# A decoder block on one core: choice weights' exponentials held together on ScalarE, their sums behind the first block's choice, and expert rows shared out anew between the stages

## The chip, the cores and the metric

The kernel runs on one core of one Trainium2 chip, in one launch. The metric is the device time of an execution in microseconds (us). A core has a TensorE (PE) for matrix products, a VectorE (DVE), a ScalarE (ACT), a GpSimd (POOL) and a SyncE (SP) that only issues transfers; each of them works through its own instructions in order and waits for the others by semaphores.

## What is computed

The block takes 512 tokens of 1024 channels. Its first half is three token mixers side by side (forgetting attention, sliding-window attention, attention to 256 memory rows), gated and merged. Its second half, where the change lies, is a retrieval of single-neuron experts:

```python
def peer_ffn(h, w_q, keys1, keys2, u, v):
    q = (h @ w_q).astype(jnp.float32).reshape(B, S, PEER_HEADS, 2, half)
    s1 = jnp.einsum('bshd,hkd->bshk', q[..., 0, :], keys1)
    s2 = jnp.einsum('bshd,hkd->bshk', q[..., 1, :], keys2)
    v1, i1 = lax.top_k(s1, PEER_TOPK)
    v2, i2 = lax.top_k(s2, PEER_TOPK)
    cand = (v1[..., :, None] + v2[..., None, :]).reshape(...)
    sv, si = lax.top_k(cand, PEER_TOPK)
    experts = e1 * N_KEYS + e2          # e1, e2: the keys behind the 16 best sums
    gates = jax.nn.softmax(sv, axis=-1)
    a = jnp.einsum('cd,ced->ce', h_c, u[e_c])
    act = jax.nn.gelu(a) * g_c
    out = jnp.einsum('ce,ced->cd', act, v[e_c])
```

Each token thus has 8 heads x 16 = 128 of 16384 experts, each with a row of u and a row of v (1024 floats).

## The kernel before

The tokens are four blocks of 128. Blocks 0 and 1 fetch their experts' rows by indirect DMA: a "row" is one expert slot for all 128 tokens of a block, a gather of 512 KB issued by POOL (L868). There are 512 of them in a fixed order: 128 u rows and 128 v rows of block 0, then the same of block 1. The function `step` handles one row and issues gathers for a few rows ahead. A u row is a product with the token and a sum on DVE (L883); a v row is scaled and added to an accumulator on DVE, which lies in SBUF (`mg`, L890) for rows beside the mixers and in PSUM (`two`, L893 and L896) for all later ones. Some rows are handled "apart": a v row is scaled on ACT (L886) and added on POOL (L887).

Blocks 2 and 3 are "dense": all 128 tiles of u and of v go through PE, and the gates are spread out to all 16384 experts. The stages follow each other like this:

1. Block 0's mixers and search; then the mixers of blocks 1 to 3, with block 0's rows beside them until `EARLY_ROWS` are done. These rows have a low priority.
2. The search of blocks 1 to 3 (`search`, L711 to L757). PE forms queries and scores of 8 heads in two halves each, 16 halves in all (scores: L754, copied to SBUF by ACT at L757); the splits `wlo` of the query weights are made by POOL (L129); POOL adds up candidates (L722); DVE finds the best 16 of three blocks for each half and then of the candidates. One row is handled each time the costs that `search` yields have added up to `PER_ROW`; every `APART`-th of them goes apart while less than `NO_APART` is spent.
3. The choice. PE runs the u tiles k=4 to 31 of the dense blocks (`dense_u`, L1029, with ACT's Gelu at L1031), with two PSUM banks. `weigh` makes the gates of blocks 1 to 3: DVE subtracts the best score (L781), ACT takes three exponentials (L784), DVE sums, inverts and multiplies (L788 to L791). `choose` finds the expert numbers of block 2, then 3, then 1, on DVE, with a row for each unit of cost (`AMONG`).
4. The spread (L1089 to L1107): 64 turns, with 60 rows among them, and u tiles. It begins with the turn of block 2's numbers and gates on PE (L1076).
5. The dense loop: 128 turns of a v tile (12 products of 512 columns), u tiles 57 to 127, and all rows that are left, shared out evenly over the first 124 turns.

Up to the end of the search a scheduler orders the instructions of all engines by its own estimate of their times. From there on POOL, DVE and PE keep the order of the code, and ACT is still ordered by the scheduler, except where `keep_in_program_order` holds an instruction.

The credit that `PER_ROW` is compared with is the same variable that `pump` sets to zero when no side work is left (L87 to L93), and each of the search's 16 weight loads calls `pump`:

```python
                cost = next(side[0], None)
...
            if cost is None:
                credit[0] = 0.0
                break
```

Of the kernel before, what the change touches and what calls it, by code (L numbers as in the profile page):

```python
# [12 lines left out]
AF = mybir.ActivationFunctionType  # L13
# [11 lines left out]
GROUPS = ((0,), (1, 2, 3))  # L25
BIG = 3
DENSE = (2, 3)
# [23 lines left out]
UNREAD = 36  # L51
LATER = 400
PACE = {"search": 20.0, "choose": 8.0, "rows": 3.5}
EARLY_ROWS, PER_ROW, APART, NO_APART = 183, 4.2, 3, 94.0


@with_exitstack
def tile_block(ctx: ExitStack, tc: tile.TileContext, t: dict, out: bass.AP):
    nc = tc.nc
    V, A, PE, G = nc.vector, nc.scalar, nc.tensor, nc.gpsimd  # L60
# [622 lines left out]
    x1, gate, acts, eidx, chosen, h2n = {}, {}, {}, {}, {}, {}  # L683
    rstd = ep.tile([128, NB], F32, name="rstd")
# [92 lines left out]
    def weigh(pool, f, g):  # L777

        nb = len(GROUPS[g])
        ex = pool.tile([128, nb, PH, TOPK], F32, name="ex")  # L780
        V.tensor_sub(ex, f.best, f.best[:, :, :, 0:1].to_broadcast([128, nb, PH, TOPK]))  # L781
        for b in range(nb):
            bf = ex[:, b].rearrange("p h s -> p (h s)")
            A.activation(bf, bf, AF.Exp, scale=rstd[:, GROUPS[g][b]:GROUPS[g][b] + 1])  # L784
        yield 0.4
        den = small.tile([128, BIG * PH], F32, tag="gden", name="gden", bufs=1)[:, :nb * PH]
        dv = den.rearrange("p (b h) -> p b h", b=nb)
        V.reduce_sum(dv, ex, axis=AX.X)  # L788
        V.reciprocal(den, den)
        for b in range(nb):  # L790
            V.tensor_mul(gates_of[g][:, b].rearrange("p s h -> p h s"), ex[:, b],  # L791
                         dv[:, b, :, None].to_broadcast([128, PH, TOPK]))
        yield 1.0

    def iota_of(pool):
        x = pool.tile([128, TOPK * NJ // 2], F32, name="iota_k")
        nc.sync.dma_start(x, t["c_iota_k"])
        return x.bitcast(BF16).rearrange("p (k s) -> p k s", k=TOPK)

    def choose(bp, f, lb, iota_k, dst):  # L800

        def new(tag, dt=F32):
            return bp.tile([128, PH, TOPK], dt, tag=tag, name=tag)

        sh, p3, p2, ri, rj = new("sh", U32), new("p3"), new("p2"), new("ri"), new("rj")
        V.tensor_scalar(sh, f.pos[:, lb], 3, None, op0=OP.logical_shift_right)
        V.tensor_scalar(p3, sh, -1.0, 0.0, op0=OP.add, op1=OP.max)
        V.tensor_scalar(sh, f.pos[:, lb], 2, None, op0=OP.logical_shift_right)
        V.tensor_copy(p2, f.pos[:, lb])
        yield 0.6  # L810
        V.scalar_tensor_tensor(p3, sh, -6.0, p3, op0=OP.add, op1=OP.max)
        V.scalar_tensor_tensor(ri, p2, -48.0, p3, op0=OP.add, op1=OP.max)
        yield 0.4
        V.tensor_scalar(rj, ri, 4.0, 24.0, op0=OP.mult, op1=OP.add)
        V.tensor_scalar(p3, ri, 8.0, 8.0, op0=OP.mult, op1=OP.add)
        V.scalar_tensor_tensor(rj, ri, 16.0, rj, op0=OP.mult, op1=OP.min)
        yield 0.6
        V.scalar_tensor_tensor(rj, ri, 48.0, rj, op0=OP.add, op1=OP.min)
        V.tensor_tensor(rj, rj, p3, op=OP.min)
        V.tensor_sub(rj, p2, rj)  # L820
        for i, r in enumerate((ri, rj)):
            yield 0.6
            rb = bp.tile([128, TOPK, PH], BF16, tag="rb", name="rb")
            V.tensor_copy(rb, r.rearrange("p h s -> p s h"))
            idb = bp.tile([128, TOPK, PH], BF16, tag="idb", name="idb")
            V.tensor_copy(idb, f.ids[i][:, lb].rearrange("p h k -> p k h"))
            hot = bp.tile([128, TOPK, TOPK, PH], BF16, tag="hot", name="hot")
            hv = hot.rearrange("p k s h -> p k (s h)")
            V.tensor_tensor(hv, rb.rearrange("p s h -> p (s h)")[:, None, :].to_broadcast([128, TOPK, NJ]),
                            iota_k, op=OP.is_equal)  # L830
            yield 1.6
            V.tensor_tensor(hot, hot, idb[:, :, None, :].to_broadcast([128, TOPK, TOPK, PH]), op=OP.mult)
            yield 1.4
            for n in (8, 4, 2):
                V.tensor_add(hv[:, :n], hv[:, :n], hv[:, n:2 * n])
            V.tensor_add(dst[i], hv[:, 0], hv[:, 1])
            yield 1.4

    def numbers_of(pool, f, lb, b, iota_k):

        g2r = pool.tile([128, D], F32, name="g2r")
        row = t["g2_row"]
        nc.sync.dma_start(g2r, bass.AP(tensor=row.tensor, offset=row.offset, ap=[[0, 128], [1, D]]))
        e = [pool.tile([128, NJ], F32, tag=f"e{i}", name=f"e{i}") for i in range(2)]
        yield from choose(pool, f, lb, iota_k, e)
        V.scalar_tensor_tensor(e[0], e[0], float(NK), e[1], op0=OP.mult, op1=OP.add)
        V.tensor_copy(eidx[b], e[0])
        if b == 0:
            h2n[0] = h2n[1] = ep.tile([128, D], F32, tag="own", name="own")
        V.scalar_tensor_tensor(h2n[b], x1[b], rstd[:, b:b + 1], g2r, op0=OP.mult, op1=OP.mult)  # L850
        yield 1.3
# [52 lines left out]
    def beside():  # L904
# [20 lines left out]
        with tc.tile_pool(name="ca", bufs=1, side="right") as pool:  # L925
            iota_k = iota_of(pool)
            yield from weigh(pool, f, 0)
            yield from numbers_of(pool, f, 0, 0, iota_k)
# [77 lines left out]
    def dense_u(k):  # L1006

        if k >= FIRST_U:
            fetch_u_to(min(max(k, PRE_U) + URING - 1, LAG) if k < LAG else k)
        w = u_raw.pop(k)  # L1010
        if split_u(k):
            if k % 2:
                hi, lo = (gp[0].tile([128, D], F32R, tag=tag, name=tag, bufs=1) for tag in ("uhi", "ulo"))
            else:
                hi, lo = halves_u[0][:, 0], halves_u[0][:, 1]
            A.copy(hi, w)
            yield
            V.tensor_sub(lo, w, hi.bitcast(F32))
            yield
            ps, hi, lo = bank("mm"), *(x.rearrange("p (n w) -> p n w", n=KC) for x in (hi, lo))  # L1020
            for dc in range(KC):
                mm3(ps[:, :TD], (hi[:, dc], lo[:, dc]), [x[dc] for x in h2s], dc == 0, dc == KC - 1)
            A.activation(ga(k), ps[:, :TD], AF.Gelu)
            return
        w = w.rearrange("p (n w) -> p n w", n=KC)
        yield
        ps = bank("mm")
        for dc in range(KC):
            PE.matmul(ps[:, :TD], w[:, dc], h2f[dc], start=dc == 0, stop=dc == KC - 1)  # L1029
            yield  # L1030
        A.activation(ga(k), ps[:, :TD], AF.Gelu)  # L1031

    f = Found(found, BIG)
# [26 lines left out]
    cp = build.enter_context(tc.tile_pool(name="cp", bufs=1))  # L1060
# [8 lines left out]
    iota_k = iota_of(cp)  # L1069

    def turn_block(i):

        ps = turned
        b = DENSE[i]
        for k, src in enumerate((*chosen[b], gate[b])):
            PE.transpose(ps[:, k * 128:(k + 1) * 128], src, ident)  # L1076
        eT = sp.tile([128, 3, 128], F32, tag="eT", name="eT", bufs=2)
        A.copy(eT.rearrange("p a b -> p (a b)"), ps[:, :384])
        slots[i] = eT
# [96 lines left out]

    NBAT = ND * 128 // GT
    PER = 128 // GT
    while k_u < FIRST_U + COVER:
        if k_u == FIRST_U + UNWEIGHED:  # L1180
            list(weigh(cp, f, 1))
        list(dense_u(k_u))
        k_u += 1
    ahead[0] = AHEAD + MORE
    credit[0] = 0.0
    for job in (*(choose(cp, f, lb, iota_k, chosen[DENSE[lb - 1]]) for lb in (1, 2)), numbers_of(cp, f, 0, 1, iota_k)):
        for cost in job:
            credit[0] += cost
            while credit[0] >= AMONG and done[0] < known[0]:
                credit[0] -= AMONG  # L1190
                step()
# [11 lines left out]
    for n in range(AHD, NBAT + AHD):  # L1203
# [8 lines left out]
        while credit[0] >= 1.0 and done[0] < known[0]:  # L1212
            credit[0] -= 1.0
            step(apart=done[0] % 4 == 0)
        if (n + 4) % PER == 0 and n + 4 < NBAT:
            turn_block((n + 4) // PER)
        spread(n - AHD)
# [139 lines left out]
```

## Time and profile before

| | us |
|---|---|
| median of 3 runs (lowest, highest) | 1583.12 (1581.81, 1583.77) |
| the profiled execution | 1584.12 |
| its span in the profile | 1582.3 |
| PE busy | 1512.7 (96%) |
| DVE busy | 1422.0 (90%) |
| ACT busy | 819.9 (52%) |
| POOL busy | 789.2 (50%) |
| transfers | 531.90 MB, mean 336 GB/s |

The profile is one execution recorded by the chip. Busy time is the union of an engine's instructions; a group names the line of the code, the engine, the tile written and the tiles read. In a timeline each row has its start and length, how many instructions it merges (x), and in brackets how long the engine was idle before and what released it. PE is near full in every stage, so single waits of a few us at the borders between stages are what such a profile is searched for.

### The profile page before, as it was taken

What the parts mean: (1) busy time and instruction counts of PE and PEld (TensorE: products, weight loads), DVE (VectorE), ACT (ScalarE), POOL (GpSimd) and SP (SyncE); (2) the same over time, 40 slices, a digit from 0 to 9 for tenths busy, and PEclk for the clock granted to TensorE, in tenths of its full rate; (3) what the DMA queues carried; (4) which work ended last, traced back from release to release, by engine and by line L of the source; (5) the groups of instructions that cost most, each with busy time, mean ns of one, the idle gap of its engine ahead of it and who ended that gap; (6) DMA issues with size and microseconds to landing.
All of it is one profiled execution on the core that took longest, in us unless ns stands there. A gap on an engine that the chain in (4) does not pass through costs nothing.

```text
span 1582.3 us, 27174 instructions
## 1 busy us (share of the span) xinstructions
PE 1512.7 (96%) x9458; PEld 1373.8 (87%) x9458; DVE 1422.0 (90%) x2661; ACT 819.9 (52%) x1831; POOL 789.2 (50%) x643
## 2 busy tenths in 40 slices
PE   8999899999999989999998999899999999999998
PEld 7989899998898989898787898688888888888887
DVE  6678487888999999999899999799999999999997
ACT  7778336646345533452215998554454454444442
POOL 1100015767576456977444665445555554555451
PEclk9999999999999999999999999999999999999999
DMA  8677657898998899987798999999999999999995
GB/s 319 212 252 251 236 197 251 307 368 310 326 348 309 280 342 337 321 307 250 240 401 303 375 396 386 347 399 390 408 409 409 410 410 407 408 406 404 408 409 193
DMA packets 178361, 531.90 MB, mean 336 GB/s; under 512 B 17456, under 2 KB 46384, under 8 KB 178224
## 3 DMA queue, kind: packets, MB, share of 16 engines
q0 software_dynamic: 73728, 268.47, 44.9%
q1 hardware_dynamic: 94416, 225.95, 39.3%
q10 hardware_dynamic: 10080, 35.75, 5.7%
q8 instruction: 74, 1.21, 0.3%
q14 instruction: 63, 0.52, 0.1%
HBM read 515.42 MB, written 14.68 MB: 335 GB/s over the span
## 4 chain that ended last, share of the span: by engine, by line
PE 58%; DVE 14%; issue 10%; DMA 10%; POOL 5%; ACT 2%; POOLq 0%; SPq 0%; DVEq 0%; ACTq 0%
PE mm L1029 9%; PE mm L146 9%; PE mm L145 9%; PE mm L147 9%; DMA row<-in_peer_v_dram,eidx 6%; POOL row L868 5%; PE sc L1104 3%; DVE two L896 2%; DVE wlo L131 2%; DMA row<-in_peer_u_dram,eidx 2%; PE sc L147 2%; PE sc L146 2%; PE tp L145 2%; PE tp L146 2%; PE sc L145 2%
## 5 line engine op out<-in xcount | busy, mean ns | idle before, releaser
L868 POOL DMA_INDIRECT row<-in_peer_v_dram,eidx x256 | 328.9, 1285 | 289.2 <-DVE two L896 164.1
L868 POOL DMA_INDIRECT row<-in_peer_u_dram,eidx x256 | 316.9, 1238 | 236.3 <-DVE scr L883 115.4
L131 DVE TENSOR_TENSOR wlo<-raw,whi 128x1024 fp32r<-128x1024 f32 (+1 forms) x228 | 278.1, 1221 | 34.2 <-ACT whi L119 30.0
L896 DVE SCALAR_TENSOR_TENSOR two<-row,acts,two 128x1024 f32<-128x1024 f32 x189 | 242.5, 1283 | 4.1 <-DMA row<-in_peer_v_dram,eidx 1.9
L119 ACT CAST whi<-raw 128x1024 fp32r<-128x1024 f32 x146 | 152.6, 1050 | 105.6 <-PE mm L146 59.7
L883 DVE SCALAR_TENSOR_TENSOR scr<-row,own 128x1024 bf16<-128x1024 f32 x128 | 156.2, 1220 | 19.0 <-DMA row<-in_peer_u_dram,eidx 17.9
L883 DVE SCALAR_TENSOR_TENSOR scr<-row,two 128x1024 bf16<-128x1024 f32 x116 | 140.9, 1215 | 5.1 <-DMA row<-in_peer_u_dram,eidx 4.3
L203 POOL TENSOR_TENSOR rsy<-rsv,mhalf 128x4 f32<-128x4 f32 (+5 forms) x25 | 38.6, 1546 | 185.6 <-DVE rsv L202 184.2
L1157 ACT CAST ah<-ga 128x256 fp32r<-128x256 f32 x116 | 47.0, 407 | 158.1 <-PE tp L146 123.8
L147 PE MATMUL mm<-hhi,wlo 128*128 128x384 f32 x320 | 110.6, 346 | 4.5 <-POOL wlo L129 4.5
L145 PE MATMUL mm<-hhi,whi 128*128 128x384 f32 x320 | 111.5, 348 | 1.6 <-ACT hhi L237 1.2
L146 PE MATMUL mm<-hlo,whi 128*128 128x384 f32 x320 | 111.9, 350 | 0.0
L1159 ACT CAST whi<-raw 128x1024 fp32r<-128x1024 f32 x96 | 100.3, 1047 | 16.1 <-DMA raw<-in_peer_v_dram 11.4
L146 PE MATMUL sc<-wlo,ah 128*128 128x512 f32 x256 | 101.2, 395 | 6.3 <-DVE wlo L131 6.3
L145 PE MATMUL mm<-whi,hhi 128*128 128x256 f32 (+1 forms) x360 | 103.7, 290 | 2.9 <-DVE g L604 1.9
L146 PE MATMUL mm<-wlo,hhi 128*128 128x256 f32 (+1 forms) x360 | 102.6, 286 | 1.5 <-DVE wlo L131 1.5
L147 PE MATMUL mm<-whi,hlo 128*128 128x256 f32 (+1 forms) x360 | 101.9, 285 | 0.8 <-DVE hlo L662 0.8
L147 PE MATMUL sc<-whi,al 128*128 128x512 f32 x256 | 101.6, 397 | 0.0
L145 PE MATMUL tp<-whi,ah 128*128 128x512 f32 x256 | 101.0, 395 | 0.0
L145 PE MATMUL sc<-whi,ah 128*128 128x512 f32 x256 | 101.0, 395 | 0.0
L146 PE MATMUL tp<-wlo,ah 128*128 128x512 f32 x256 | 100.9, 394 | 0.0
L147 PE MATMUL tp<-whi,al 128*128 128x512 f32 x256 | 100.6, 393 | 0.0
(323 smaller groups left out, 4527.8 us busy)
## 6 DMA issues: line engine op xcount, KB each, us to landing
raw<-in_peer_v_dram SPq DMA_DIRECT2D x96, 512.0 KB
hhi<-in_uT_dram ACTq DMA_DIRECT2D x68, 512.0 KB
raw<-in_w_tr_dram SPq DMA_DIRECT2D x48, 512.0 KB
raw<-in_w_nat_dram SPq DMA_DIRECT2D x40, 512.0 KB
last<-in_peer_v_dram SPq DMA_DIRECT2D x32, 512.0 KB
hhi<-in_uT_dram SPq DMA_DIRECT2D x26, 512.0 KB
raw<-in_w_o_dram SPq DMA_DIRECT2D x24, 512.0 KB
gd<-st SPq DMA_DIRECT2D x24, 512.0 KB
```

The lines of the kernel that those rows point to most:

```text
L119: (cast or A.copy)(hi[:, :n * w], raw[:, :n * w])
L131: V.tensor_sub(lo, raw, hi.bitcast(F32))
L145: PE.matmul(ps, lh, rh, start=first, stop=False)
L146: PE.matmul(ps, lh, rl, start=False, stop=False)
L147: PE.matmul(ps, ll, rh, start=False, stop=last)
L868: G.indirect_dma_start(out=r, out_offset=None, in_=t["peer_" + tab], in_offset=bass.IndirectOffsetOnAxis(ap=eidx[b][:, j:j + 1], axis=0))
L883: V.scalar_tensor_tensor(scr, r, 1.0, two[0] if b else h2n[b], op0=OP.mult, op1=OP.mult, accum_out=acts[b][:, c]))
L896: V.scalar_tensor_tensor(two[0], r, acts[b][:, c], two[0], op0=OP.mult, op1=OP.add))
L1029: PE.matmul(ps[:, :TD], w[:, dc], h2f[dc], start=dc == 0, stop=dc == KC - 1)
L1104: PE.matmul(ps[:, u], o[:, 1, u], o[:, 0, u], start=True, stop=True)
L1157: A.copy(ah, a)
L1159: A.copy(hi, raw)
```

## The change

Three edits:

- `EARLY_ROWS` goes from 183 to 176, `PER_ROW` from 4.2 to 3.4 and `APART` from 3 to 4.
- In `weigh`, the second and third exponential are held in program order on ACT, right behind the first.
- `weigh` is no longer run out at once. Its first part (the subtraction and the exponentials) stands where it stood, before u tile 18 in the code; its second part (sums, reciprocal, products) comes behind `choose` of block 2, and now counts as a cost for the rows.

```diff
-EARLY_ROWS, PER_ROW, APART, NO_APART = 183, 4.2, 3, 94.0
+EARLY_ROWS, PER_ROW, APART, NO_APART = 176, 3.4, 4, 94.0
...
-            A.activation(bf, bf, AF.Exp, scale=rstd[:, GROUPS[g][b]:GROUPS[g][b] + 1])
+            ins = A.activation(bf, bf, AF.Exp, scale=rstd[:, GROUPS[g][b]:GROUPS[g][b] + 1])
+            if b:
+                tc.keep_in_program_order(ins)
...
+    weighing = weigh(cp, f, 1)
     while k_u < FIRST_U + COVER:
         if k_u == FIRST_U + UNWEIGHED:
-            list(weigh(cp, f, 1))
+            next(weighing)
         list(dense_u(k_u))
         k_u += 1
...
-    for job in (*(choose(cp, f, lb, iota_k, chosen[DENSE[lb - 1]]) for lb in (1, 2)), numbers_of(cp, f, 0, 1, iota_k)):
+    for job in (choose(cp, f, 1, iota_k, chosen[DENSE[0]]), weighing, choose(cp, f, 2, iota_k, chosen[DENSE[1]]),
+                numbers_of(cp, f, 0, 1, iota_k)):
```

Because each weight load throws the credit away, the search does not get the 31 rows that 105.6 units of cost at 3.4 would give. Counted in the built programs, the rows are shared out so:

| rows | before | after |
|---|---|---|
| beside the mixers | 183 | 176 |
| in the search (DVE + apart) | 24 (17 + 7) | 26 (20 + 6) |
| in the choice, all on DVE | 36 | 37 |
| done when the spread begins | 243 | 239 |
| in the spread | 60 | 60 |
| left for the dense loop | 209 | 213 |

Line numbers of the changed kernel are higher by 2 behind L784 and by 4 behind L1188. All engines' orders are the same up to the start of the search. There, DVE before has seven of the rows beside the mixers (`mg<-row`) between the last work of the mixers and the first searches (MAX, MAX_INDEX and MATCH_REPLACE on the scores `s`); five of the seven are seen here:

```order
L1044 COPY rstd<-rsy 128x3
L890 SCALAR_TENSOR_TENSOR mg_2288<-row,acts_207,mg_2288 128x1024
L711 MAX v_7904<-s 128x8 x3
L712 MAX_INDEX ids_7609<-v_7904,s 128x8
L713 MATCH_REPLACE tmp<-v_7904,s 128x128
L890 SCALAR_TENSOR_TENSOR mg_2288<-row,acts_207,mg_2288 128x1024
L712 MAX_INDEX ids_7609<-v_7904,s 128x8 x2
L714 MAX v_7904<-tmp 128x8
L715 MAX_INDEX ids_7609<-v_7904,tmp 128x8
L890 SCALAR_TENSOR_TENSOR mg_2288<-row,acts_207,mg_2288 128x1024
L711 MAX v_7904<-s 128x8 x3
L890 SCALAR_TENSOR_TENSOR mg_2288<-row,acts_207,mg_2288 128x1024
```

On DVE at the same place in the changed kernel the first searches stand alone:

```order
L1046 COPY rstd<-rsy 128x3
L711 MAX v_7883<-s 128x8 x3
L712 MAX_INDEX ids_7588<-v_7883,s 128x8
L713 MATCH_REPLACE tmp<-v_7883,s 128x128
L712 MAX_INDEX ids_7588<-v_7883,s 128x8 x2
L714 MAX v_7883<-tmp 128x8
L715 MAX_INDEX ids_7588<-v_7883,tmp 128x8
L711 MAX v_7883<-s 128x8 x3
```

The seven rows are gone from there; the search has three more of the form `two<-row` on DVE, farther back, and one less apart.

On ACT, behind the search's last copy of scores, the exponentials (`ex<-ex`, each kind of function behind its ACT_TABLE_LOAD) stand among the Gelus of the u tiles (`ga<-mm`). Before:

```order
L757 COPY s<-sc 128x384
L886 ACTIVATE row<-row,acts_207 128x1024
L1031 ACTIVATE ga<-mm 128x256 x4
L784 ACT_TABLE_LOAD
L784 ACTIVATE ex<-ex,rstd 128x128
L1031 ACT_TABLE_LOAD
L1031 ACTIVATE ga<-mm 128x256
L784 ACT_TABLE_LOAD
L784 ACTIVATE ex<-ex,rstd 128x128 x2
L1031 ACT_TABLE_LOAD
L1031 ACTIVATE ga<-mm 128x256 x24
```

On ACT at the same place in the changed kernel:

```order
L757 COPY s<-sc 128x384
L888 ACTIVATE row<-row,acts_207 128x1024
L1033 ACTIVATE ga<-mm 128x256 x5
L784 ACT_TABLE_LOAD
L784 ACTIVATE ex<-ex,rstd 128x128 x3
L1033 ACT_TABLE_LOAD
L1033 ACTIVATE ga<-mm 128x256 x24
```

Two of the four table loads are gone, and one more Gelu, that of u tile 7, stands ahead of the exponentials.

On POOL in the second half of the search, the splits `wlo` of the query weights stand among gathers, candidates and rows apart (`mg<-mg,row`). Before:

```order
L129 TENSOR_TENSOR wlo<-raw,whi 128x1024
L868 DMA row<-in_peer_v_dram,eidx_206 128x1024 x3
L887 TENSOR_TENSOR mg_2288<-mg_2288,row 128x1024
L722 TENSOR_TENSOR cand<-v_8540 128x3x24
L722 TENSOR_TENSOR cand<-v_8540 128x3x16
L129 TENSOR_TENSOR wlo<-raw,whi 128x1024
```

On POOL at the same two splits in the changed kernel:

```order
L129 TENSOR_TENSOR wlo<-raw,whi 128x1024
L722 TENSOR_TENSOR cand<-v_8367 128x3x8
L889 TENSOR_TENSOR mg_2288<-mg_2288,row 128x1024
L870 DMA row<-in_peer_v_dram,eidx_206 128x1024
L722 TENSOR_TENSOR cand<-v_8367 128x3x16
L870 DMA row<-in_peer_v_dram,eidx_206 128x1024 x2
L722 TENSOR_TENSOR cand<-v_8518 128x3x24
L722 TENSOR_TENSOR cand<-v_8518 128x3x16
L129 TENSOR_TENSOR wlo<-raw,whi 128x1024
```

Here the two programs do nearly the same between the splits; from the search's start to its last split POOL has four gathers and one row apart less than before (13 gathers and 2 rows apart against 17 and 3).

## The prediction

> **What bounds the kernel now.** I read the page's span first, then the busy time in stretches that I cut at the borders of the stages.
>
> ```profile
> span 1582.3 us, 27174 instructions
> ...
> core 0: us, PE busy (x) PEld busy (x) DVE busy (x) ACT busy (x) POOL busy (x), PEclk, DMA share, GB/s
> ...
> 700.00:730.00 30.00, 26.46 (x140) 25.73 (x140) 29.93 (x177) 8.88 (x15) 27.91 (x25) 0.89 0.56 197
> ...
> 760.00:848.00 88.00, 81.71 (x371) 71.37 (x371) 81.30 (x129) 15.86 (x33) 41.31 (x39) 0.98 0.89 337
> 848.00:985.00 137.00, 134.56 (x841) 123.93 (x842) 130.20 (x193) 123.34 (x461) 82.83 (x67) 0.99 0.98 363
> 985.00:1060.00 75.00, 65.43 (x358) 54.67 (x357) 61.35 (x97) 41.34 (x92) 34.54 (x28) 1.00 0.98 370
> 1060.00:1200.00 140.00, 140.00 (x831) 123.96 (x830) 135.32 (x194) 67.62 (x100) 72.50 (x54) 1.00 1.02 403
> 1200.00:1550.00 350.00, 344.55 (x1998) 302.07 (x1997) 345.15 (x359) 167.95 (x247) 178.50 (x130) 1.00 1.03 408
> ```
>
> Each row is a stretch: its length, each engine's busy time, PE's granted clock, the transfers' share and rate. PE and DVE are both nearly full all along. The search (646 to 759) is full on DVE (29.93 of 30 us in 700 to 730), the choice (to 848) leaves some 6.5 us idle on each of the two, and the dense loop is full on both, with transfers at 408 GB/s. Time is to be had only where PE and DVE get free together, and that is around the exponentials. The timelines of DVE, ACT and PE there:
>
> ```profile
> 758.84 0.55 DVE L781 TENSOR_TENSOR ex<-best 128x384 f32<-128x384 f32 x1
> 764.96 0.55 DVE L788 TENSOR_REDUCE gden<-ex 128x24 f32<-128x384 f32 x1 [5.57 <-ACT ex L784]
> ...
> 752.32 0.38 ACT L1031 ACTIVATE ga<-mm 128x256 f32<-128x256 f32 x1 [3.07 <-PE mm L1029]
> 759.53 1.28 ACT L784 ACT_TABLE_LOAD   x1 [6.83 <-DVE ex L781]
> 760.83 0.40 ACT L784 ACTIVATE ex<-ex,rstd 128x128 f32<-128x128 f32 x1
> ...
> 762.54 0.38 ACT L1031 ACTIVATE ga<-mm 128x256 f32<-128x256 f32 x1
> 762.94 1.28 ACT L784 ACT_TABLE_LOAD   x1
> 764.24 0.69 ACT L784 ACTIVATE ex<-ex,rstd 128x128 f32<-128x128 f32 x2
> ...
> 766.24 0.38 ACT L1031 ACTIVATE ga<-mm 128x256 f32<-128x256 f32 x1
> 768.42 0.39 ACT L1031 ACTIVATE ga<-mm 128x256 f32<-128x256 f32 x1 [1.79 <-PE mm L1029]
> ...
> 738.31 20.89 PE L1029 MATMUL mm<-h2f,ga 128*128 128x256 f32 x96
> 762.98 1.46 PE L1029 MATMUL mm<-h2f,ga 128*128 128x256 f32 x5 [3.78 <-ACT ga L1031]
> ```
>
> DVE stands still for 5.57 us until ACT has all three exponentials. ACT, waiting 6.83 us for DVE, holds back the Gelus behind it, and PE, with two banks, stops for 3.78 us. From the Gelu at 752.32 to that at 768.42 are three u tiles of 3.45 us (3.07 idle and 0.38 in ACT's undisturbed rows), so PE loses 16.1 - 10.4 = 5.7 us, the last 2 of them at a lower clock. Which of the two the spread waits for is seen at its start:
>
> ```profile
> 844.20 0.38 PE L1076 MATMUL tp<-cst,e 128*128 128x128 f32 x2
> ...
> 845.31 0.48 ACT L1078 COPY eT<-tp 128x384 f32<-128x384 f32 x1 [0.53 <-DVE own L850]
> ...
> 847.59 3.48 DVE L1089 TENSOR_TENSOR o<-tp,eT 128x1024 f32<-128x1024 f32 x3
> ```
>
> The numbers for it are ready at 845.8 (PE's way), DVE comes at 847.6: DVE sets the end, and PE's way is only 1.8 us shorter. A gain on DVE alone is worth at most 1.8 us, one on PE alone nothing.
>
> **The search.** Seven rows of the old form leave its front. These are the five that lie behind the first scores:
>
> ```profile
> 650.40 2.17 DVE L890 SCALAR_TENSOR_TENSOR mg<-row,acts,mg 128x1024 f32<-128x1024 f32 x1
> 653.60 3.32 DVE L890 SCALAR_TENSOR_TENSOR mg<-row,acts,mg 128x1024 f32<-128x1024 f32 x1
> 657.43 3.85 DVE L890 SCALAR_TENSOR_TENSOR mg<-row,acts,mg 128x1024 f32<-128x1024 f32 x1
> 662.53 1.26 DVE L890 SCALAR_TENSOR_TENSOR mg<-row,acts,mg 128x1024 f32<-128x1024 f32 x1
> 664.63 1.26 DVE L890 SCALAR_TENSOR_TENSOR mg<-row,acts,mg 128x1024 f32<-128x1024 f32 x1
> ...
> 649.23 0.68 DVE L711 MAX8 v<-s 128x8 f32<-128x128 f32 x3 [1.20 <-ACT qp L750]
> ...
> 757.66 1.27 DVE L896 SCALAR_TENSOR_TENSOR two<-row,acts,two 128x1024 f32<-128x1024 f32 x1
> ```
>
> They take 11.9 us; the other two lie ahead of DVE's wait for scores that ends at 649.23, and are worth nothing. Three more rows come at 1.18 us (757.66 to the next at 758.84): 3.5 us. That would be 8.4 us less, if DVE never waited for scores. But PE makes them at its own pace. I added up DVE's instructions of the search at the pitches of this trace, no half ahead of its scores: in the order of before this ends at 758.8, as measured; in the new order at 757.4 if PE's scores come when they do now, 8.2 us of it waiting, most of it in the second half. So the gain hangs on PE:
>
> ```profile
> 669.14 0.45 PE L147 MATMUL mm<-hhi,wlo 128*128 128x384 f32 x1 [1.01 <-POOL wlo L129]
> ...
> 713.62 0.69 PE L147 MATMUL mm<-hhi,wlo 128*128 128x384 f32 x1 [3.54 <-POOL wlo L129]
> 714.10 0.52 PE L145 MATMUL mm<-hhi,whi 128*128 128x384 f32 x1
> 714.42 0.52 PE L146 MATMUL mm<-hlo,whi 128*128 128x384 f32 x1
> ...
> 699.61 0.23 POOL L722 TENSOR_TENSOR cand<-v 128x24 f32<-128x24 f32 x1 [2.77 <-DVE v L714]
> 699.80 2.40 POOL L887 TENSOR_TENSOR mg<-mg,row 128x1024 f32<-128x1024 f32 x1
> ```
>
> PE waits 1.01 and 3.54 us for POOL's splits, and after the second its pitch is 0.32 us (714.10 to 714.42) instead of 0.17, for 18 products: 2.6 us more. POOL in turn is late because it waits in its queue for DVE (2.77 us at 699.61), and through the rows apart. In the new order DVE is some 8 us ahead at that point, and POOL has one row apart (2.40 us) and four gathers less in its way. I take it that all of these waits go: PE's last scores end at 738.3 - 1.0 - 3.5 - 2.6 = 731.2, and my sum for DVE then gives 753 for the end of the search. Bounds: 752.7 and 757.4.
>
> The slow clock is a rule of the Trainium skill too ("TensorE: Matmul & The Clock Gate", on the HAM clock gate): an idle window of about 3.4 us halves PE's clock, and a busy one brings it back. The trace agrees, at 3.54 and at 3.78 us idle, while 1.01 us did nothing. By the rule the 2.6 us go with the wait; without it PE would end its scores at 733.8, and the sum would be 0.5 us worse.
>
> **The choice.** On DVE it now takes 847.59 - 758.84 = 88.75 us. The 5.57 us go, since the first block's choice stands behind the subtraction, and ACT needs only some 4 us; the sums are still made, later. One row more (37, not 36) costs 1.2. So it ends at 753 + 84.4 = 837.4: 10.2 us earlier. On PE: 731.2, 29 tiles of 3.45 us, and what is lost at the exponentials. They now hold ACT for two loads (2.56), 1.09 and a Gelu, to about 757.7; PE has filled both banks at 731.2 + 7 x 3.45 = 755.4, so it still waits 2.3 us. It ends at 833.7 where it ended at 844.2 (the transposition of the numbers), and these are ready 1.6 us later as now, at 835.3, 2.1 us ahead of DVE. Cover is thus there for both; if the search ends at 757.4, DVE starts the spread at 841.8, a gain of 5.8.
>
> **The spread** keeps its 60 rows, four more of them v and four less u. It is covered: PE is busy 134.56 of 137 us, and the two forms take about the same (below). I take 0.
>
> **The dense loop** gets 213 rows instead of 209.
>
> ```profile
> L896 DVE SCALAR_TENSOR_TENSOR two<-row,acts,two 128x1024 f32<-128x1024 f32 x127 | 163.2, 1285 | 3.7 <-DMA row<-in_peer_v_dram,eidx 1.9
> ...
> L883 DVE SCALAR_TENSOR_TENSOR scr<-row,two 128x1024 bf16<-128x1024 f32 x85 | 103.4, 1216 | 5.1 <-DMA row<-in_peer_u_dram,eidx 4.3
> ```
>
> These are groups of the loop's instructions: busy time, mean ns of one, idle time before. A row is 1.22 (u) or 1.28 us (v) of DVE, so four cost 5.1 us where DVE sets the pace and 0 where PE does. In 985 to 1200 PE is full or DVE has slack (4.7 us in 1060 to 1200): nothing. In 1200 to 1550 neither has over 5.5 us, and there lie 350 of the loop's 565 us (985 to 1550), so 2.5 of the rows: 3.2 us. I take that; bounds 0 and 5.1.
>
> **Sum**, against the profiled execution's 1584.1 (span 1582.3 and 1.8 around it): -10.2 + 3.2 = -7.0, 1577.1. That execution is 1.0 above the median of 1583.1, so I predict 1576.1 for the median; the rivals' times are on the median too.
>
> **The rivals.**
> - *PE's scores come no earlier.* POOL finds another thing to wait for. For it: POOL is busy 27.91 of 30 us around the wait. Then -5.8 + 3.2: 1580.5.
> - *PE sets the pace of the dense loop*, and the four rows cost nothing. For it: 140.00 of 140 us. Then -10.2: 1572.9.
> - *Transfers set it.* Four rows are 2.1 MB, at the 408 GB/s measured 5.1 us: 1578.0. For it: a DMA share of 1.03; against it, DVE's waits for rows are 1.9 and 4.3 us in the whole loop. The Trainium skill ("Perfetto Trace Analysis", on the roofline) puts a single core's ceiling at its 16 DMA engines, about 435 GB/s; the trace shows 408 in that stretch. By that figure I estimate 4.8 us.
> - *Slower: the ring of row buffers sets it.* A gather is issued when DVE frees a buffer, and then takes long to land (the chain of waits; and who waited for whom in 1060 to 1550: us, times, longest):
>
> ```profile
> 1329.46 9.49 DMA row<-in_peer_v_dram,eidx
> ...
> POOL row L868 <- DVE two L896: 138.4, 91, 3.3
> ```
>
>  If gather, landing and row were the loop that bounds, each row would add its whole share of the time, 565 us for 209 rows or 2.7: four rows 10.8 us. With a search that gains only 5.8, that is 5.0 slower: 1588.1. It decides from 1.5 us a row with that gain, and from 2.6 with mine. Against it stand the same short waits of DVE.
> - *The change doesn't do what it says*: 31 rows in the search. The orders of the built program exclude it; with 31, five rows at 1.18 us would make the search 6 us longer and the dense loop one row shorter than before, 1578.
>
> **How the numbers follow.** My forecast gets 0.60 (its own range 1574 to 1579), late scores 0.15, a PE-bound loop 0.10, a transfer-bound loop 0.09, the ring 0.06. What a measurement can tell from no change is about 0.2%, 3.2 us, so faster means below 1579.9. All of the first, third and fourth lie there but for a few chances in a hundred; the second lies around the bound, mostly within. Faster 0.76, same 0.18, slower 0.06. The range takes in the second and third case: 1571.5 to 1582.5.
>
> **What would show it.** Right: L781 at about 753 and no wait of 5 us behind it; PE without the 3.54 us wait and at full clock in 700 to 730; L1089 at about 837; the dense loop some 3 us longer. Wrong: an L781 above 757, PE idle over 3.4 us at the exponentials, DVE waiting for numbers at the spread's start, or a dense loop that grows by more than 5.1 us.

## The result, and the profile after

| | before | changed |
|---|---|---|
| median (lowest, highest; 6 runs each) | 1583.44 (1581.81, 1588.44) | 1573.04 (1568.66, 1576.78) |
| ratio, with its 95% interval | | 0.9947 (0.9926 to 0.9968) |
| profiled execution, its span | 1584.12, 1582.3 | 1574.62, 1572.8 |

The changed kernel is faster by 0.53%, 8.4 us of 1583. Measured once more later, the same kernel gave 0.9962 (0.9944 to 0.9980), 6.0 us; the predicted 7.0 lies between the two.

Stretches of the changed kernel, in the columns of the prediction: the second half of the search, the choice, and two of the dense loop.

```profile
700.00:730.00 30.00, 30.00 (x179) 29.20 (x178) 30.00 (x182) 9.22 (x16) 19.81 (x20) 1.00 0.54 180
760.00:838.00 78.00, 75.79 (x349) 66.55 (x347) 76.47 (x115) 8.89 (x23) 39.50 (x36) 0.99 0.98 367
...
1050.00:1190.00 140.00, 140.00 (x831) 124.09 (x830) 135.09 (x195) 68.60 (x101) 73.08 (x54) 1.00 1.02 406
1190.00:1540.00 350.00, 341.82 (x1975) 299.72 (x1974) 344.84 (x359) 165.98 (x244) 177.99 (x131) 1.00 1.03 407
```

In 700 to 730 PE had been busy for 26.46 us at a clock of 0.89; now it is busy for all 30 at 1.00, and POOL for 19.81, not 27.91. The choice lost DVE's idle time (1.5 of 78 us are left). The dense loop looks as before.

DVE's timeline at the search's start and end, at the sums and at the spread's start:

```profile
649.61 0.68 DVE L711 MAX8 v<-s 128x8 f32<-128x128 f32 x3 [4.50 <-ACT s L757]
...
653.19 0.68 DVE L711 MAX8 v<-s 128x8 f32<-128x128 f32 x3 [1.27 <-ACT s L757]
...
752.80 0.56 DVE L781 TENSOR_TENSOR ex<-best 128x384 f32<-128x384 f32 x1
...
778.23 0.55 DVE L790 TENSOR_REDUCE gden<-ex 128x24 f32<-128x384 f32 x1
...
836.77 4.61 DVE L1091 TENSOR_TENSOR o<-tp,eT 128x1024 f32<-128x1024 f32 x4
```

The first search starts where it did (649.23 before), the subtraction comes 6.0 us earlier, the sums wait for nothing, and the spread starts at 836.77, not 847.59: 10.8 us. ACT and PE meanwhile:

```profile
747.36 0.38 ACT L1033 ACTIVATE ga<-mm 128x256 f32<-128x256 f32 x1 [3.07 <-PE mm L1031]
753.51 1.28 ACT L784 ACT_TABLE_LOAD   x1 [5.76 <-DVE sh L808]
754.80 0.98 ACT L784 ACTIVATE ex<-ex,rstd 128x128 f32<-128x128 f32 x3
755.80 1.28 ACT L1033 ACT_TABLE_LOAD   x1
757.10 0.66 ACT L1033 ACTIVATE ga<-mm 128x256 f32<-128x256 f32 x2
762.98 0.38 ACT L1033 ACTIVATE ga<-mm 128x256 f32<-128x256 f32 x1 [5.22 <-PE mm L1031]
...
835.87 0.48 ACT L1080 COPY eT<-tp 128x384 f32<-128x384 f32 x1
```

```profile
729.22 0.83 PE L754 MATMUL sc<-keys,qp 128*128 128x128 f32 x6
...
757.53 12.31 PE L1031 MATMUL mm<-h2f,ga 128*128 128x256 f32 x48 [3.31 <-ACT ga L1033]
```

ACT's three exponentials stand together between one pair of table loads, but ACT still waits 5.76 us for DVE ahead of them, and PE still stops for 3.31 us. The next three tiles take 12.31 us instead of 3 x 3.45 = 10.35. The numbers for the spread are ready at 835.87 + 0.48 = 836.35, only 0.42 us ahead of DVE.

### The profile page after: what moved, and what is told of

Same layout as the page of the kernel before. It is cut to its first block, busy times and chain, and to the rows that moved or that the text cites. A ratio compares the mean times of both kernels' runs of the same rounds, so it can differ in the third digit from the quotient of the medians.

```text
span 1572.8 us, 27174 instructions
## 1 busy us (share of the span) xinstructions
PE 1505.7 (96%) x9458; PEld 1366.9 (87%) x9458; DVE 1418.6 (90%) x2663; ACT 814.2 (52%) x1827; POOL 782.3 (50%) x642
## 4 chain that ended last, share of the span: by engine, by line
PE 53%; DVE 14%; DMA 13%; issue 11%; POOL 6%; ACT 2%; POOLq 0%; DVEq 0%; ACTq 0%
PE mm L1031 9%; PE mm L146 8%; PE mm L147 8%; PE mm L145 8%; POOL row L870 6%; DMA row<-in_peer_v_dram,eidx 5%; DMA row<-in_peer_u_dram,eidx 4%; PE sc L1106 3%; DVE wlo L131 2%; DVE two L898 2%; PE mm L746 2%; PE sc L146 1%; PE sc L147 1%; PE sc L145 1%; PE tp L145 1%
## 5 line engine op out<-in xcount | busy, mean ns | idle before, releaser
L870 POOL DMA_INDIRECT row<-in_peer_v_dram,eidx x256 | 322.0, 1258 | 293.2 <-DVE two L898 176.0
L898 DVE SCALAR_TENSOR_TENSOR two<-row,acts,two 128x1024 f32<-128x1024 f32 x196 | 251.7, 1284 | 2.8 <-DMA row<-in_peer_v_dram,eidx 0.4
L1161 ACT CAST whi<-raw 128x1024 fp32r<-128x1024 f32 x96 | 100.2, 1047 | 16.4 <-DMA raw<-in_peer_v_dram 10.8
L145 PE MATMUL mm<-whi,hhi 128*128 128x256 f32 (+1 forms) x360 | 103.2, 289 | 2.9 <-DVE g L604 1.9
```

Source lines behind the costliest of these rows:

```text
L145: PE.matmul(ps, lh, rh, start=first, stop=False)
L870: G.indirect_dma_start(out=r, out_offset=None, in_=t["peer_" + tab], in_offset=bass.IndirectOffsetOnAxis(ap=eidx[b][:, j:j + 1], axis=0))
L898: V.scalar_tensor_tensor(two[0], r, acts[b][:, c], two[0], op0=OP.mult, op1=OP.add))
L1161: A.copy(hi, raw)
```

## The experiments

Ten more kernels ran, and the changed one (after_again) once more. The table gives each one's own landmarks in its profile: the search from its first MAX to the subtraction, the choice from there to the first `o<-tp,eT`, the dense loop from its first `sc<-wlo,ah` (0.4 us behind its first product) to the end of the span, with its rows. The medians of before differ from call to call (1583.4, 1582.9, 1581.5, 1580.0), so ratios are what to compare.

| kernel | median | ratio (95%) | search | choice | loop (rows) |
|---|---|---|---|---|---|
| before | 1583.44 | 1 | 109.61 | 88.75 | 577.2 (209) |
| changed | 1573.04 | 0.9947 (0.9926 to 0.9968) | 103.19 | 83.97 | 580.8 (213) |
| after_again | 1573.58 | 0.9962 (0.9944 to 0.9980) | 103.20 | 85.30 | 577.8 (213) |
| numbers_only | 1579.26 | 0.9965 (0.9949 to 0.9981) | 103.20 | 85.56 | 579.8 (214) |
| weigh_only | 1581.95 | 0.9993 (0.9978 to 1.0009) | 109.64 | 86.44 | 575.1 (208) |
| early_only | 1573.25 | 0.9937 (0.9911 to 0.9963) | 99.43 | 85.34 | 580.1 (215) |
| search_only | 1578.83 | 0.9987 (0.9966 to 1.0008) | 116.04 | 84.17 | 571.8 (206) |
| kept_credit | 1577.07 | 0.9966 (0.9951 to 0.9980) | 107.68 | 84.31 | 578.2 (208) |
| late_exps | 1573.45 | 0.9962 (0.9945 to 0.9978) | 99.46 | 84.16 | 582.7 (215) |
| rows_16_fewer | 1559.81 | 0.9865 (0.9839 to 0.9892) | 103.20 | 85.21 | 567.3 (197) |
| rows_16_more | 1595.79 | 1.0086 (1.0054 to 1.0118) | 103.21 | 85.32 | 599.9 (229) |
| dve_16_more | 1596.69 | 1.0076 (1.0057 to 1.0094) | 103.20 | 83.99 | 601.1 (213) |
| loop_apart | 1583.78 | 1.0022 (1.0006 to 1.0039) | 103.20 | 85.30 | 590.6 (213) |

The search's length is the same to 0.03 us wherever the program of the search is the same (seven profiles of the changed numbers). The search can thus be judged by one profile. The other stages repeat less well: the two profiles of the changed kernel differ by 1.3 us in the choice and by 3.0 us in the loop, so smaller differences there say little, and a total is judged by its median.

**The change in two parts.** numbers_only has the three numbers and the old `weigh`; weigh_only the new `weigh` and the old numbers:

```diff
 numbers_only
+EARLY_ROWS, PER_ROW, APART, NO_APART = 176, 3.4, 4, 94.0
             list(weigh(cp, f, 1))
 weigh_only
+EARLY_ROWS, PER_ROW, APART, NO_APART = 183, 4.2, 3, 94.0
             next(weighing)
```

> Only the three numbers (176, 3.4, 4); weigh as before. As in the changed kernel, the three exponentials stand together, in the built order too. My theory (the rows' new shares shorten the search and put the exponentials together; the split of weigh adds only what DVE then waits for them): the subtraction L781 at 753, as in the changed kernel, DVE's wait behind it 2 to 3 us (one table load and three exponentials) and not 5.6, the spread begins at 838 to 839 on DVE, total 7 to 9 us under before (ratio 0.9945 to 0.9955). Rival (the two edits share the gain about equally, the wait stays at 5.6): spread at 841 to 842, total 3 to 5 us under before.

> Only weigh's two edits, with the old numbers (183, 4.2, 3). The orders of PE, POOL and SP are those of before, and the exponentials stay apart on ACT, two loads more, despite the hold. My theory (PE's way is only 1.8 us shorter than DVE's, so DVE's 5.57 us alone are worth at most that): no DVE wait behind L781, DVE done with the choice at 843, but the spread begins at 845.5 to 846.5, when PE's numbers come; total 2 to 3 us under before (one row less in the dense loop), ratio 0.998 to 0.999. Rival (the edits add up): spread at 843, total 5 us under, ratio 0.997.

The numbers alone shorten the search to the full 103.20. Behind it DVE still waits (DVE of numbers_only):

```profile
759.23 0.56 DVE L781 TENSOR_TENSOR ex<-best 128x384 f32<-128x384 f32 x1
762.24 0.55 DVE L788 TENSOR_REDUCE gden<-ex 128x24 f32<-128x384 f32 x1 [2.46 <-ACT ex L784]
```

The wait is 2.46 us, not 5.57: the exponentials stand together here too, without the hold. With the old numbers and the hold, in weigh_only, they stay apart, with four table loads. So the numbers bring them together, in the order that the scheduler gives ACT; the hold does not. The subtraction's place at 759.23 instead of 753 says nothing against the mechanism: the mixers of that execution ended 6.4 us later (first MAX at 656.03, not 649.61). Counted from the first MAX the spread starts after 188.8 us, as expected. In the time the numbers gave less than expected: 0.9965, some 5.5 us, where 7 to 9 were to come.

In weigh_only DVE's 5.57 us go and come back in part (DVE at the spread's start):

```profile
842.43 1.29 DVE L898 SCALAR_TENSOR_TENSOR two<-row,acts,two 128x1024 f32<-128x1024 f32 x1
845.68 2.36 DVE L1091 TENSOR_TENSOR o<-tp,eT 128x1024 f32<-128x1024 f32 x2 [1.97 <-ACT eT L1080]
```

DVE comes earlier and then waits 1.97 us for the turned numbers: the spread starts 1.9 us earlier than before, as "worth at most 1.8" had it, and the whole kernel is the same within the interval (0.9993; 0.998 to 0.999 was expected). In its profile the spread took 161.2 us instead of 157.5; the runs don't show why.

**Which of the numbers shortens the search.** early_only takes only the seven rows from the front; search_only only has more rows in the search.

```diff
 early_only
+EARLY_ROWS, PER_ROW, APART, NO_APART = 176, 4.2, 3, 94.0
 search_only
+EARLY_ROWS, PER_ROW, APART, NO_APART = 183, 3.4, 4, 94.0
```

> Only EARLY_ROWS goes to 176; PER_ROW 4.2 and APART 3 stay those of the kernel before, the two edits at weigh stay as in the changed kernel. In the built order the seven rows are gone from the search's front, the search has 17 rows on DVE and 7 apart (changed kernel: 20 and 6), the exponentials stand together, and the dense loop keeps 215 rows. My theory (the search is DVE's instructions, once PE's scores are not late): from the first search MAX to the subtraction 103.2 - 3 x 1.18 = 99.7 us (99.5 to 100.5), no wait for the exponentials; the spread starts some 80.4 + 83.9 us after the first MAX; two more rows in the loop cost 2 to 2.4 us, so the time is 0 to 2 us under the changed kernel, 1571 to 1573 (0.993 to 0.995 of before). Rival 1 (the search's end is set by PE's scores, which the seventh row apart on POOL delays): 102.5 to 104 us, and PE waits over 2 us for a split. Rival 2 (the front rows gave nothing by themselves, PER_ROW and APART did): 107 us or more.

> Only PER_ROW 3.4 and APART 4 are changed; EARLY_ROWS stays 183, the two edits at weigh stay as in the changed kernel. In the built order the seven rows stand again in the search's front, the search has 20 rows on DVE and 6 apart, the exponentials stand together, and the dense loop has 206 rows. My theory (the five front rows are full price on DVE when PE's scores are prompt): from the first MAX to the subtraction 103.2 plus up to 11.9, less the 1.3 us of waits that they fill: 111 to 114 us; a choice of 84 us without a wait; the dense loop 6 to 8 us shorter than the changed kernel's 577; in all 1.5 to 5 us over the changed kernel, 1575 to 1578 (0.995 to 0.997 of before). Rival (the late scores alone set the search of the kernel before, and the rows in front fill time in which DVE waits): 103 to 106 us, and then the time is under that of the changed kernel by 3 us or more, since the loop has seven rows less.

The front rows alone give 109.61 - 99.43 = 10.2 us, and the three more rows cost 103.19 - 99.43 = 3.8, 1.25 each. The theory holds in early_only's search (99.43 for 99.7); PE waits for no split there, although seven rows go apart as in the kernel before. Its profile is of the slowest of its five runs, 1582.88 for a median of 1573.25: the mixers ended late (first MAX at 653.46) and the spread took 162.7 us, for no reason that the runs show. In search_only PE waits for POOL again (0.99 and 2.15 us), so the late splits belong to the rows in front, not to the rows apart. Its 116.04 us are 2 above the range, and its ratio, 0.9987, is above the 0.995 to 0.997 expected, for a reason that I had not seen (ACT, then DVE, of search_only):

```profile
731.17 0.38 ACT L1033 ACTIVATE ga<-mm 128x256 f32<-128x256 f32 x1 [2.98 <-PE mm L1031]
742.73 1.15 ACT L888 ACTIVATE row<-row,acts 128x1024 f32<-128x1024 f32 x1 [11.17 <-DMA row<-in_peer_v_dram,eidx]
743.78 0.46 ACT L757 COPY s<-sc 128x384 f32<-128x384 f32 x1
```

```profile
744.27 0.68 DVE L711 MAX8 v<-s 128x8 f32<-128x128 f32 x3 [2.82 <-ACT s L757]
```

On ACT the last copy of scores stands behind the scaling of a row apart. That row's gather landed late, ACT stood for 11.17 us, and DVE waited 2.82 us for scores that PE had long made. The changed kernel has the same order there and got through with 0.39 us.

Nearly half of what the front rows cost is due to POOL: three of the five take 5.6 us more than 1.26 each. Three of POOL's splits in the kernel before, to be laid beside the five rows that the prediction shows:

```profile
649.06 2.41 POOL L129 TENSOR_TENSOR wlo<-raw,whi 128x1024 fp32r<-128x1024 f32 x1
...
653.40 2.43 POOL L129 TENSOR_TENSOR wlo<-raw,whi 128x1024 fp32r<-128x1024 f32 x1
...
657.78 2.42 POOL L129 TENSOR_TENSOR wlo<-raw,whi 128x1024 fp32r<-128x1024 f32 x1
```

The splits end at 651.47, 655.83 and 660.20; the rows of 2.17, 3.32 and 3.85 us end at 652.57, 656.92 and 661.28, each 1.1 us behind a split, a little less than the length that a row has alone (1.26). By these ends, three of the five rows stood still until POOL was done. The form with its accumulator in PSUM has no such rows: the 16 in this search took 1265 to 1279 ns.

**All 31 rows in the search.** kept_credit keeps the search's credit apart from the one that the weight loads set to zero:

```diff
-            credit[0] += cost
-            while credit[0] >= PER_ROW and NJ <= done[0] < known[0]:
-                credit[0] -= PER_ROW
+            own += cost
+            while own >= PER_ROW and NJ <= done[0] < known[0]:
+                own -= PER_ROW
```

> The changed kernel with a credit of its own for the search, which the weight loads do not set to zero: the search gets all 31 rows, 24 on DVE and 7 apart, and the dense loop 208. My theory (a row costs DVE the same wherever it stands): first MAX to subtraction 103.2 + 4 x 1.18 = 107.9 us (107.5 to 109), the dense loop 577 - 5 x 1.0 = 572 (570.5 to 573), so within 2 us of the changed kernel (0.993 to 0.996 of before). Rival (the search has room, as the late scores left it): 103 to 105 us, and 3 to 5 us under the changed kernel.

The search's 107.68 is as expected: four rows, 4.5 us. The loop's 578.2 is not the 572 expected: against the two profiles of the changed kernel, five rows fewer gave between -0.4 and 2.6 us. That is less than the 1.1 us that a row costs in the search, but two profiles of one kernel already differ by 3.0 us here. The ratio, 0.9966, just misses the 0.993 to 0.996 expected; it is worse than 0.9947 and 0.9962, though the intervals overlap.

**What sets the dense loop.** Three kernels change its load. rows_16_more handles 16 v rows of block 1 twice, dve_16_more makes only DVE's instruction of 16 v rows twice, rows_16_fewer leaves 16 v rows out:

```diff
 rows_16_more
+    JOBS[-1:-1] = [(1, "v", j) for j in range(NJ - 17, NJ - 1)]
 dve_16_more
+            for _ in range(2 if b and NJ // 4 <= j < NJ // 4 + 16 else 1):
 rows_16_fewer
+    del JOBS[-17:-1]
```

> The changed kernel with 16 v rows of block 1 handled twice (their gather and their DVE instruction), so block 1's output is not the reference's; 229 rows in the dense loop instead of 213. DVE or transfers set the loop: 16 x 1.28 = 20 us over the changed kernel. As the step from 209 to 213 rows showed (3.6 us, 0.9 a row): 14 us. PE sets it: under 5 us. The ring of buffers sets it: 16 x 2.7 = 43 us.

> The changed kernel with DVE's instruction of 16 v rows of block 1 made twice, without a second gather (block 1's output is not the reference's): 20 us more DVE work in the dense loop and no more transfers. If DVE sets the loop, it gets as much longer as in rows_16_more, 14 to 20 us; if transfers set it, 0 to 5 us.

> The changed kernel with 16 of the 128 v rows of block 1 left out (neither gathered nor added), so the dense loop has 197 rows, not 213. It tells what sets the loop below the changed kernel's load. DVE sets it all through: 16 x 1.19 = 19 us less, loop 558 us. My theory (DVE, with PE close behind: busy 558 of 578 us, and some 12 us of its idle time lie in the start and the end of the loop): 9 to 16 us less. PE sets it: 4 us or less. The ring of row buffers sets it (2.7 us a row): over 25 us less.

Upwards a row costs 1.2 to 1.4 us (599.9 against 580.8 and 577.8), and DVE's instruction alone costs as much, without a byte of transfer more. So above the changed kernel's load neither the transfers nor the ring of buffers sets the loop. Downwards a row gives 0.7 to 0.8 (567.3). A straight line through the loops of all ten profiles with 197 to 215 rows gives 0.78 us a row, with kept_credit 2.5 us above it, the farthest of them. The stretch of the loop shows why, first in dve_16_more, then in rows_16_fewer:

```profile
1190.00:1540.00 350.00, 329.99 (x1862) 286.34 (x1862) 346.21 (x358) 155.38 (x228) 168.72 (x125) 0.98 0.99 384
```

```profile
1190.00:1540.00 350.00, 349.63 (x2054) 308.78 (x2053) 342.72 (x365) 171.64 (x251) 167.51 (x122) 1.00 1.01 400
```

With more on DVE, PE has 20 us to spare; with 16 rows less PE is full, 349.63 of 350. The changed kernel's 341.82 (PE) and 344.84 (DVE) lie at the crossing.

**Rows away from DVE.** If DVE sets the loop, rows handled on POOL and ACT should shorten it. loop_apart sends every 16th of the loop's rows there:

```diff
-            step()
+            step(apart=done[0] % 16 == 5)
```

> The changed kernel with 13 of the dense loop's 213 rows (every 16th) handled apart: multiplied on POOL and summed on ACT (5 u rows), or scaled on ACT and added on POOL (8 v rows), as the spread does it already; the gathers are the same. PE, SP and the order of gathers are unchanged, DVE has 13 instructions of 1.2 us less in the loop. My theory (DVE sets the loop, PE is close behind with 558 of 578 us busy): the loop becomes 5 to 12 us shorter than 577, and the kernel 1561 to 1568 (0.986 to 0.991 of before). Rival 1 (the ring of row buffers sets it: POOL waits in its queue for the row that goes apart, and the gathers behind it are late): no gain, or up to 10 us slower than the changed kernel. Rival 2 (transfers set it): within 2 us of the changed kernel.

Its loop became 10 to 13 us longer (590.6), the opposite of the theory. Rival 1 gives the size, and its reason is a part: of the 10.2 us by which the span is longer, 5.6 are idle time of DVE, and its waits for rows rose from 6.4 to 11.1 us. The larger part of what the theory missed stands in DVE's groups from 995 to 1570, of the changed kernel and of loop_apart:

```profile
L131 DVE TENSOR_TENSOR wlo<-raw,whi 128x1024 fp32r<-128x1024 f32 x95 | 115.9, 1220 | 4.4 <-ACT whi L1161 3.5 <-ACT ah L1159 0.7
...
L1164 DVE TENSOR_TENSOR al<-ga,ah 128x256 fp32r<-128x256 f32 x115 | 48.2, 419 | 0.9 <-ACT ah L1159 0.9
...
L131 DVE TENSOR_TENSOR wlo<-last,whi 128x1024 fp32r<-128x1024 f32 x32 | 39.0, 1220 | 0.5 <-ACT whi L1161 0.5
```

```profile
L131 DVE TENSOR_TENSOR wlo<-raw,whi 128x1024 fp32r<-128x1024 f32 x95 | 119.0, 1252 | 5.0 <-ACT whi L1161 4.1 <-ACT ah L1159 0.9
...
L1164 DVE TENSOR_TENSOR al<-ga,ah 128x256 fp32r<-128x256 f32 x113 | 55.9, 494 | 0.0
...
L131 DVE TENSOR_TENSOR wlo<-last,whi 128x1024 fp32r<-128x1024 f32 x31 | 43.1, 1391 | 0.0
```

Thirteen rows of 1.2 us went from DVE, 16 us, yet from 995 to the end DVE was busy for 559.5 us instead of 554.9: its other instructions took 20 us more. To the end of the span, the five groups of splits (`wlo`, `al`, `u` and `ulo`) went from 288.5 to 308.2 us, as many instructions as before; the rows' own instructions, which read `two` in PSUM, kept their means (1284 ns for 1286, 1215 for 1218). One place, DVE and then POOL:

```profile
1103.34 1.22 DVE L131 TENSOR_TENSOR wlo<-raw,whi 128x1024 fp32r<-128x1024 f32 x1
1104.48 2.63 DVE L1164 TENSOR_TENSOR al<-ga,ah 128x256 fp32r<-128x256 f32 x1
```

```profile
1104.26 2.57 POOL L880 TENSOR_TENSOR row<-row,own 128x1024 f32<-128x1024 f32 x1
```

A subtraction of 0.42 us took 2.63 and ended at 1107.11, 0.28 us behind POOL's row (1106.83). It is what the front rows of the search showed: a DVE instruction that reads two tiles in SBUF stands until POOL's has ended. In the loop DVE makes many such splits, so rows on POOL take more from DVE (20 us for 13) than they relieve it of (16).

**PE's way through the choice.** early_only's spread waits for PE (first line below); late_exps adds to it that ACT comes to the exponentials two Gelus later:

```diff
-AMONG, UNWEIGHED = 1.0, 14
+AMONG, UNWEIGHED = 1.0, 5
-            if b:
-                tc.keep_in_program_order(ins)
+            tc.keep_in_program_order(ins)
-        A.activation(ga(k), ps[:, :TD], AF.Gelu)
+        ins = A.activation(ga(k), ps[:, :TD], AF.Gelu)
+        if FIRST_U <= k < FIRST_U + COVER:
+            tc.keep_in_program_order(ins)
```

> early_only (EARLY_ROWS 176, PER_ROW 4.2, APART 3) with the three exponentials and the Gelus of u tiles 4 to 31 held in program order on ACT and UNWEIGHED 5, so that two more Gelus stand ahead of the exponentials (six, not four) and ACT comes to them when DVE's subtraction is just done. In early_only PE stops for 3.00 us there and DVE then waits 1.10 us for the turned numbers at the spread's start. My theory (there the spread waits for PE, and PE's loss at the exponentials comes from ACT waiting for DVE): PE's stop falls to 1.5 us or less, the wait of 1.10 us goes, and the spread starts 183.4 us after the search's first MAX (182.8 to 184.2) instead of 184.8; the kernel is 0 to 2 us under early_only, 1571 to 1573 (0.992 to 0.994 of before). Rival (DVE sets the spread's start, and the 1.10 us stand for something else): 184.8 us, no change. Rival 2 (exponentials too late, DVE's sums wait for them): a wait of over 2 us at the sums and a start after 186 us.

The start of the spread on DVE in early_only; then, in late_exps, the search's end and the start of the spread on DVE, and ACT at the exponentials:

```profile
838.23 4.61 DVE L1091 TENSOR_TENSOR o<-tp,eT 128x1024 f32<-128x1024 f32 x4 [1.10 <-ACT eT L1080]
```

```profile
750.85 0.55 DVE L781 TENSOR_TENSOR ex<-best 128x384 f32<-128x384 f32 x1
...
835.01 4.61 DVE L1092 TENSOR_TENSOR o<-tp,eT 128x1024 f32<-128x1024 f32 x4
```

```profile
752.58 0.38 ACT L1032 ACTIVATE ga<-mm 128x256 f32<-128x256 f32 x1 [3.07 <-PE mm L1030]
752.98 1.28 ACT L784 ACT_TABLE_LOAD   x1
```

ACT no longer waits, PE has no stop there at all, and the spread starts 183.6 us after the first MAX instead of 184.8, without a wait. The mechanism is as expected. In the time it can't be seen: 0.9962, the same as the changed kernel beside it, where 0.992 to 0.994 was expected. Its spread starts 3.5 us sooner than the changed kernel's (187.2 after the first MAX). Against that, in the profiles, stand a spread of 158.5 us (155.2 and 156.1 in the changed kernel) and a loop of 582.7 with two more rows (580.8 and 577.8). Both differences are about as large as those between executions of one program, so whether the earlier start is lost there or hidden by noise stays open.

**The same kernel again.**

> The changed kernel once more, nothing edited, for a second profile and more times. My theory (the stages' lengths belong to the program, while the mixers and the spread differ from execution to execution): from the first search MAX to the subtraction 103.2 us again (103.1 to 103.3), a choice of 83.9 to 85.4; but the first MAX anywhere from 646 to 656 (649.61 in the first profile), and from the spread's start to the dense loop's first product 155 to 159 us, so that the 2.3 us by which this was shorter than before are not the change's. Rival (the spread is shorter by the change): 155.2 us again, within 0.4. The ratio: 0.9925 to 0.9955 of before.

The search took 103.20 again; the first MAX came at 651.17. The ratio, 0.9962, is just above the 0.9925 to 0.9955 expected. The choice took 85.30 instead of 83.97, and the waits on DVE name the cause, a wait that only some executions have:

```profile
DVE hot L831 <- DMA iota_k<-in_c_iota_k_dram: 1.2, 1, 1.2
```

From the spread's start to the loop's first `sc<-wlo,ah`: 156.1 us, 155.2 in the first profile, 157.5 in before. The four kernels that change only the loop gave 156.2, 157.0, 157.5 and 158.5 there. So the changed program takes 155 to 158.5, and before lies within that.

## Why the prediction was right

- **Bound.** That DVE sets the start of the spread, with PE's way just behind, held: weigh_only won only 1.9 us of the 5.57, and early_only, with DVE 3.8 us earlier, ran into PE.
- **The search.** Predicted end 753, measured 752.80. That the two agree to 0.2 us is in part luck, since the first MAX moves by several us between executions; what repeats is the length, 103.2 us, where the prediction amounts to 753 - 649.23 = 103.8. The parts: front rows 10.2 net (11.9 were in the rows, some of them in time that DVE now waits in, 1.27 us at 653.19), three rows 3.8 for 3.5. PE's waits for the splits and the slow clock went, as taken; its last scores end at 730.05 for 731.2. Of the reasons given for POOL, the one that carried is DVE being ahead; the row apart less was not needed. The gathers that go with the front rows were not tried apart from them. "PE's scores come no earlier" falls with this.
- **The choice.** Predicted 84.4, measured 83.97, and 85.30 with the wait for `iota_k`. Here the exact size of one term failed: PE's margin was to be 2.1 us and was 0.42. The term "it still waits 2.3 us" was too small: since PE's scores were 1.1 us earlier still, its two banks were full at 754.2, and the stop was 3.31 us. That is also long enough for the slow clock, which costs 2.0 us more and which the step had left out. That it cost nothing was luck: DVE was still later, but only by 0.42.
- **The spread.** Predicted 0; the profile showed 2.3 us less, which the repeats put down to executions, not to the change.
- **The dense loop.** Predicted 3.2 for four rows; 3.6 in the first profile and 0.6 in the second. Two profiles can't settle that. Sixteen rows fewer give 0.7 to 0.8 a row and the line through ten profiles 0.78, which makes 3 for four. The picture behind it, DVE and PE both close, was right: DVE sets it above 213 rows, and below, PE takes over in the middle of the loop. Of the rivals the PE-bound loop is half true, downwards; transfers and ring fall above this load with dve_16_more, and below it 0.7 to 0.8 us a row is less than the 1.3 and 2.7 that they would cost.
- **31 rows in the search** was a rival at 1578, and kept_credit measured 1577.07 (0.9966, which is 1577.7 on the median of 1583.1). The changed kernel has 26 such rows.
- **Sum.** -10.2 + 3.2 = -7.0 was forecast; -8.4 and -6.0 were measured. By the runs apart, most of it is in the numbers (0.9965), the moved sums add some 1.6 us to them (the spread starts 188.8 us behind the first MAX in numbers_only, 187.2 in the changed kernel), and alone they are worth nothing measurable.

Not tried: the changed kernel with the last copy of scores ahead of the row apart on ACT. What order it would take to make the late gather harmless stays open.

## What to carry to other kernels

Price a row, or any movable piece of work, at the place where it stands: the same row cost about 2 us in front of the search, 1.1 to 1.25 in it, and 0.7 to 1.4 in the dense loop, and most of the gain came from this difference. Where two engines are both nearly full, a gain on one shows at the next border only as far as the other's margin reaches, so work out both arrival times there first. Before moving work from DVE to POOL, look what DVE reads meanwhile.

## What the runs showed of the hardware

- **DVE behind POOL.** DVE instructions with two tiles in SBUF took 2.2 to 3.9 instead of 1.3 us, or 2.63 instead of 0.42, and ended 1.1 and 0.28 us behind POOL's subtraction or product of 2.4 to 2.6 us. With one operand in PSUM the mean stayed at 1284 ns (`two<-row`, 119 in loop_apart's loop, 1286 for 127 in the changed kernel). The Trainium skill ("SBUF — State Buffer", section "SBUF: two separate sides") has the rule: the two engines share a pair of ports as an exclusive lock for a whole instruction, which a DVE operation with two inputs in SBUF needs too when POOL's reads SBUF. The traces agree by the ends. Who comes first they don't show cleanly: the row at 657.43 starts 0.35 us ahead of its split at 657.78 and still ends behind it.
- **PE's slow clock.** Stops of 3.31 to 3.33 us were followed by it in seven profiles, with 12.0 to 13.6 us for three tiles instead of 10.35 (granted clock 0.87 from 757 to 770 in the changed kernel); stops of 3.00, 2.95 and 2.10 us were not (granted clock 1.00 right behind them). The Trainium skill ("TensorE: Matmul & The Clock Gate", Part 1) puts the window at about 3.4 us and calls it free-running; the traces have the limit between 3.00 and 3.31 in this place, as the profile counts idle time, and a different length of the slow part, 12.31 and 13.64, for the same stop in two executions.
- **Executions differ in the mixers.** The first MAX of the search lay anywhere from 646.9 to 656.0 us in profiles whose programs are the same up to there, while the search behind it repeated to 0.03 us.
